# One row of each partition of a block stored by itself, in transfers of 125 and 3 partitions that only the first five DMA engines move

## The chip, the cores and the metric

The kernel runs on one core of a Trainium2 chip. The metric is the time of the kernel on the device in microseconds (us), lower is better. Times are medians over several executions, and a comparison uses executions of both kernels on the same chip in the same rounds. The ratios given are the mean time of the fast runs of one kernel over that of the other's of the same rounds, so they are not quite the ratios of the medians that stand beside them.

## The reference

A linear layer with an adapted and normalized weight (DoRA), in float32; `x` has 16 x 2048 rows of 256 numbers and `W` is 256 x 256:

```python
W_adapted = W + scale * (lora_A @ lora_B)
W_norm = np.sqrt(np.sum(W_adapted ** 2, axis=0, keepdims=True) + 1e-8)
W_final = W_adapted / W_norm * m
y = x.reshape(-1, in_dim) @ W_final
```

Nearly all of the cost is reading `x` (33.6 MB) and writing `y` (33.6 MB).

## The kernel before

The rows of `x` are cut into 8 blocks of 4096. A block lies in SBUF as 128 partitions with 32 rows of 1 KB each, in one of five buffers. Loads go out from SyncE (SP), stores from ScalarE (ACT); each of the two issues into a queue of its own, and both queues run on the same 16 DMA engines. A chunk is 4 rows of each partition. GpSimd rounds two chunks to bfloat16, TensorE transposes and multiplies, VectorE and ACT empty the accumulators, and ACT writes `y` over the chunk of `x` and issues a store when enough chunks are done.

The stores, as (first chunk, chunks, rows in one transfer, chunk after whose drain it is issued); here `F` is 3, `G` is 24, `CH` is 8 and `J` is 4:

```python
stores = [(b * CH, CH, CH * J, 19 + b) for b in range(F - 1)]
stores += [(G - CH, 3, 3 * J, G), (G - 5, 5, 5 * J, G)]
FIRST = len(stores)
stores += [(G, 4, J, G + 3), (G + 4, 1, J, G + 4)]
stores += [(G + 5, CH - 5, (CH - 5) * J, 44), (G + CH, CH, CH * J, 44)]   # the first of these is changed
stores += [(b * CH, CH, CH * J, (b + 1) * CH - 1) for b in range(F + 2, NBLK - 1)]
stores += [(g0, cnt, cnt * J, g0 + cnt - 1) for g0, cnt in units[-2:]]
# ... (cut)
for r in range(0, cnt * J, rows):                                          # in transfer()
    here = x_bufs[b % XBUFS][:, c * J + r : c * J + r + rows, :]
    there = unit[:, (g0 - u0) * J + r : (g0 - u0) * J + r + rows, :]
    src, dst = (here, there) if store else (there, here)
    engine.dma_start(out=dst, in_=src).then_inc(sem(name), 16)
```

## Time and profile before

| | before |
|---|---|
| time, median | 162.64 us (162.43 to 163.18, 3 runs) |
| span of the profiled execution | 161.3 us |
| moved | 33.85 MB read, 33.55 MB written, 418 GB/s on the mean |
| compute ends (last store issued) | 131.15 us |
| last byte of the last store | 160.74 us |

The kernel is bound by its transfers: the DMA engines are full from start to end, and the last 30 us are stores that wait in the queue. Its time is therefore the time at which the last of the 16 DMA engines is done. The lines that show this are in the prediction below.

### The profile page before, as it was taken

How to read it: one execution, taken by the hardware profiler on the slowest of the kernel's cores; microseconds unless marked ns; L12 is line 12 of the kernel's file. 1: busy time of each engine (PE TensorE's matmuls, PEld its weight loads, DVE VectorE, ACT ScalarE, POOL GpSimd, SP SyncE). 2: the span in 40 equal slices, each digit the busy share in tenths (PEclk: the TensorE clock that was granted, in tenths of full speed). 3: DMA queues.
4: the chain of work that ended last, by engine and by line, in shares of the span. 5: the costliest groups of instructions: out<-in, count | busy, mean ns of one | idle time of the engine just before them, and what ended most of it. 6: DMA issues, size and time to landing. Idle time of an engine off the chain costs nothing. (4 is left out here: it accounts for less than half of the span.)

```text
span 161.3 us, 2027 instructions
## 1 busy us (share of the span) xinstructions
PE 96.0 (60%) x786; PEld 84.8 (53%) x786; DVE 45.0 (28%) x44; ACT 66.0 (41%) x68; POOL 60.9 (38%) x38
## 2 busy tenths in 40 slices
PE   0795936999999720000799999989997920000000
PEld 0384925899998610000689999979977910000000
DVE  0667421435353500000214445335443300000000
ACT  3311740686777450000057676777774640000000
POOL 1045319668685000002938676755829000000000
PEclk9999996999999985555569999999999997555555
DMA  4999999999999999989999999999999999999995
GB/s 167 425 457 455 390 512 398 390 512 398 423 390 480 398 463 426 431 365 453 423 403 444 407 437 427 422 423 430 443 483 398 423 473 408 406 480 415 386 443 219
DMA packets 4645, 67.43 MB, mean 418 GB/s; under 512 B 657, under 2 KB 674, under 8 KB 1698
## 3 DMA queue, kind: packets, MB, share of 16 engines
q1 hardware_dynamic: 2304, 33.82, 49.2%
q10 hardware_dynamic: 2338, 33.59, 48.9%
q14 instruction: 3, 0.02, 0.0%
HBM read 33.85 MB, written 33.55 MB: 418 GB/s over the span
## 5 line engine op out<-in xcount | busy, mean ns | idle before, releaser
L276 ACT COPY x_sb<-y_ps 128x1024 f32<-128x1024 f32 x64 | 62.2, 1015 | 58.8 <-PE y_ps L335 57.1
L208 POOL CAST xb<-x_sb 128x2048 bf16<-128x2048 f32 x31 | 58.4, 1893 | 63.5 <-DMA x_sb<-in_x_dram 24.8
L335 PE MATMUL y_ps<-w_final,xt 128*128 128x256 bf16 x512 | 64.1, 279 | 3.9 <-PEq L311 3.8
L248 DVE COPY xt<-xt_ps 128x1024 f32<-128x1024 f32 x32 | 39.1, 1224 | 75.1 <-PE xt_ps L321 75.0
L335 PEld LDWEIGHTS y_ps<-w_final,xt 128*128 128x128 bf16 x512 | 51.0, 100 | 11.5 <-issue 4.9
L321 PE MATMUL xt_ps<-identity,xb 128*128 128x128 f32 x264 | 37.5, 290 | 24.9 <-PEq L311 24.9
L321 PEld LDWEIGHTS xt_ps<-identity,xb 128*128 128x128 f32 x264 | 32.8, 151 | 26.4 <-issue 25.9
L292 PE MATMUL y_ps<-identity,a_nat 128*16 128x128 f32 x2 | 0.6, 398 | 4.2 <-DMA a_nat<-in_lora_A_dram 4.2
L264 ACT CAST xb<-x_sb 128x2048 bf16<-128x2048 f32 x1 | 1.9, 1898 | 2.6 <-DMA x_sb<-in_x_dram 2.6
L292 PEld LDWEIGHTS y_ps<-identity,a_nat 128*16 128x16 f32 x2 | 0.1, 88 | 4.1 <-issue 4.1
L262 ACT ACT_TABLE_LOAD x1 | 1.3, 1283 | 2.4 <-issue 2.4
L238 DVE RECIPROCAL rnorm<-norm 128x256 f32<-128x256 f32 x1 | 1.8, 1752 | 1.3 <-ACT norm L268 1.3
L305 PE MATMUL y_ps<-sq,ones 128*128 128x256 f32 x4 | 2.1, 675 | 0.0
L214 POOL MEMSET xb<- 128x2048 bf16 x1 | 1.8, 1805 | 0.0
L305 PEld LDWEIGHTS y_ps<-sq,ones 128*128 128x128 f32 x4 | 1.2, 324 | 0.8 <-DVE sq L229 0.7
L301 PE MATMUL y_ps<-m_row,ones 1*128 1x256 f32 x2 | 1.2, 710 | 0.5 <-DMA m_row<-in_m_dram 0.5
L220 DVE CAST b_bf<-b_nat 16x256 bf16<-16x256 f32 x1 | 0.3, 281 | 3.3 <-DMA b_nat<-in_lora_B_dram 3.3
L301 PEld LDWEIGHTS y_ps<-m_row,ones 1*128 1x128 f32 x2 | 0.5, 305 | 1.0 <-DMA m_row<-in_m_dram 1.0
L268 ACT ACTIVATE norm<-y_ps,eps_col 128x256 f32<-128x256 f32 x1 | 0.5, 476 | 1.2 <-PE y_ps L305 1.2
L225 DVE SCALAR_TENSOR_TENSOR wa<-y_ps,w_nat 128x512 f32<-128x512 f32 x1 | 0.7, 692 | 0.8 <-PE y_ps L296 0.8
L296 PE MATMUL y_ps<-b_bf,aT 16*128 16x256 bf16 x2 | 0.6, 400 | 0.5 <-DVE aT L222 0.5
L241 DVE TENSOR_TENSOR w_final<-wam,rnorm 128x256 bf16<-128x256 f32 x2 | 0.8, 422 | 0.0
(14 smaller groups left out, 3.7 us busy)
## 6 DMA issues: line engine op xcount, KB each, us to landing
out_dram<-x_sb ACTq DMA_DIRECT2D x5, 4096.0 KB, 27.2
x_sb<-in_x_dram SPq DMA_DIRECT2D x7, 2048.0 KB, 29.6
x_sb<-in_x_dram SPq DMA_DIRECT2D x3, 4096.0 KB, 29.9
out_dram<-x_sb ACTq DMA_DIRECT2D x2, 2048.0 KB, 30.3
x_sb<-in_x_dram SPq DMA_DIRECT2D x1, 3072.0 KB, 46.1
out_dram<-x_sb ACTq DMA_DIRECT2D x2, 1536.0 KB, 19.3
out_dram<-x_sb ACTq DMA_DIRECT2D x1, 2560.0 KB, 30.7
out_dram<-x_sb ACTq DMA_DIRECT2D x5, 512.0 KB, 38.1
```

The source lines that it names most:

```text
L208: nc.gpsimd.tensor_copy(out=xb_bufs[p % NXB][:], in_=x_bufs[b % XBUFS][:, 2 * c * J : 2 * (c + 1) * J, :],).then_inc(sem("rounded"), 1)
L214: nc.gpsimd.memset(xb_bufs[NPR % NXB][:], 0.0).then_inc(sem("rounded"), 1)
L238: nc.vector.reciprocal(out=rnorm[:], in_=norm[:]).then_inc(dv, 1)
L241: i = nc.vector.tensor_mul(out=w_final[:, t], in0=wam[:, t], in1=rnorm[:])
L248: nc.vector.tensor_copy(out=xt_bufs[p % NXT][:].rearrange("p r t -> p (r t)").bitcast(FP32), in_=xt_ps[p % 2][:],).then_inc(sem("copied"), 1)
L262: nc.scalar.activation(out=warm[:], in_=eps_col[:], func=AF.Sqrt)
L264: nc.scalar.copy(out=xb_bufs[0][:], in_=x_bufs[0][:, 0 : 2 * J, :]).then_inc(sem("early"), 1)
L276: nc.scalar.copy(out=x_bufs[b % XBUFS][:, c * J : (c + 1) * J, :], in_=y_ps[g % 2][:]).then_inc(sem("room"), 1)
L301: nc.tensor.matmul(mb_ps, ones[0:1, :], m_row[:], start=True, stop=True).then_inc(pe, 1)
L305: i = nc.tensor.matmul(n2_ps, ones[:], sq[:, t, :], start=(t == 0), stop=(t == KC - 1))
L321: i = nc.tensor.transpose(xt_ps[p % 2][:, j * P : (j + 1) * P], xb_bufs[p % NXB][:, j, :].bitcast(FP32), identity[:],)
L335: i = nc.tensor.matmul(y_ps[h][:, j, :], xt_bufs[p % NXT][:, r : r + P, t], w_final[:, t, :], start=(t == 0 and (j % (J // 2)) == 0), stop ...
```

## The change

Its intent is to even out the ends of the DMA engines. The store of the last three chunks of block 3 has 12 rows in each partition. The twelfth row is taken out of it and stored in two transfers, of partitions 0 to 124 and 125 to 127. A transfer of 125 partitions is moved by five engines only, one of 3 partitions by three, so 128 KB that all 16 engines shared now lie on the first five.

```diff
+    ODD = FIRST + 2
...
     def pieces(entry):
+        if entry is stores[ODD]:
+            return 16 * 3
         return 16 * (entry[1] * J // entry[2])
...
-            engine.dma_start(out=dst, in_=src).then_inc(sem(name), 16)
+            parts = [(0, P, 0, rows)]
+            if (g0, cnt, rows) == stores[ODD][:3]:
+                parts = [(0, P, 0, rows - 1), (0, 125, rows - 1, 1), (125, 3, rows - 1, 1)]
+            for p0, n, r0, k in parts:
+                engine.dma_start(
+                    out=dst[p0 : p0 + n, r0 : r0 + k, :],
+                    in_=src[p0 : p0 + n, r0 : r0 + k, :],
+                ).then_inc(sem(name), 16)
```

## The prediction

> **What bounds the kernel now.** I read the page first: the span, the forty slices, the DMA queues and the chain that ended last.
>
> ```profile
> span 161.3 us, 2027 instructions
> ...
> PE   0795936999999720000799999989997920000000
> ...
> DMA  4999999999999999989999999999999999999995
> GB/s 167 425 457 455 390 512 398 390 512 398 423 390 480 398 463 426 431 365 453 423 403 444 407 437 427 422 423 430 443 483 398 423 473 408 406 480 415 386 443 219
> ...
> HBM read 33.85 MB, written 33.55 MB: 418 GB/s over the span
> ```
>
> The 16 DMA engines are full from the second slice to the last but one. TensorE is empty in the last seven slices, so compute is done at about 131 us and the last 30 us are stores alone. The chain that ended last covers only a few per cent of the span for the same reason: the thing waited for at the end is a queue of transfers. The kernel moves 67.4 MB and cannot be shorter than the time in which its most loaded DMA engine moves its sixteenth. So for this change the only question is which DMA engine ends last, and by how much.
>
> Next I read the tail in a table of windows. The two columns that matter are the last two: mean share of the 16 engines that is busy, and GB/s. A packet is counted in the window in which it starts, so one of 1 us can show more than 1.00.
>
> ```profile
> 157.00:158.00 1.00, 0.00 (x0) 0.00 (x0) 0.00 (x0) 0.00 (x0) 0.00 (x0) 0.50 0.92 393
> 158.00:159.00 1.00, 0.00 (x0) 0.00 (x0) 0.00 (x0) 0.00 (x0) 0.00 (x0) 0.50 1.11 475
> 159.00:159.50 0.50, 0.00 (x0) 0.00 (x0) 0.00 (x0) 0.00 (x0) 0.00 (x0) 0.50 0.39 164
> 159.50:160.00 0.50, 0.00 (x0) 0.00 (x0) 0.00 (x0) 0.00 (x0) 0.00 (x0) 0.50 0.08 33
> 160.00:161.30 1.30, 0.00 (x0) 0.00 (x0) 0.00 (x0) 0.00 (x0) 0.00 (x0) 0.50 0.03 13
> ```
>
> In the last window 0.03 x 1.3 us x 16 engines = 0.62 us: a single packet of 16 KB (611 ns each in the trace) on a single engine. All other engines are already empty. So there is a **straggler**, one of sixteen.
>
> To size it I used the packet records of the trace (start, duration, bytes; the engine is not recorded). In steady state a packet starts 3 or 4 ns before the previous packet of the same engine ends, and each engine must get its share of every transfer in order, so the records can be linked into 16 chains. This is my reconstruction, but it leaves almost no gap unexplained. The chains end at 159.26, 159.30, 159.31, 159.34, 159.35, 159.40, 159.45, 159.49, 159.49, 159.50, 159.65, 159.71, 159.74, 159.99, 160.02 and 160.74 us; the mean is 159.61. Perfect balance would therefore be worth 160.74 - 159.61 = 1.13 us (0.7% of 162.64), which caps any gain from moving bytes between engines. The straggler's lead over the next is 0.72 us. Its 32 KB store packets averaged 1240 ns against the normal 1213 ns, in long runs of slow packets (49 to 57 us and 116 to 136 us); it is slow again and again, not hit once. The two at 160.0 got there by a few isolated long packets or by one 303 ns gap. The chain that also carried the one-partition load of m ends at 159.35.
>
> **What the Trainium skill says.** "DMA: Bandwidth & Descriptors", section "Why a DMA increments its semaphore by 16 and not by 1": a transfer issued from SP or ACT uses the largest k up to 16 that divides the slowest dimension, on the lowest-numbered k engines; the unused 16 - k increments come at once. So 125 partitions go to engines 0 to 4 with 25 rows each, and 3 partitions to engines 0 to 2 with one each. The wait for 3 x 16 remains right. The trace of before has only even transfers and the one-partition load, so it shows no more than that this load's 1 KB packet was one packet. The same page, "Latency and other measured facts": engines 7 and 15 are usually slower than the rest in traces, with a guess at a cause tied to the software path. The trace agrees that one engine is slow in the stores (1240 against 1213 ns) though nothing here uses that path; it can't tell which number it has. The same page, "Why small descriptors are slow": each packet has a fixed overhead. The trace agrees: a 1 KB packet takes 46 ns, 4 KB takes 159, 12 KB takes 460, 16 KB takes 611; that is about 37.7 ns per KB plus 8 ns.
>
> **The change part by part.** The transfer concerned is the store of the last three chunks of block 3 (12 rows of 1 KB in each partition, 1.5 MB), issued when the 45th chunk is drained.
>
> ```profile
> 104.49 0.86 ACTq L146 DMA_DIRECT2D out_dram<-x_sb  x2
> 104.80 0.86 PEld L335 LDWEIGHTS y_ps<-w_final,xt 128*128 128x128 bf16 x8
> ...
> 105.39 1.93 ACT L276 COPY x_sb<-y_ps 128x1024 f32<-128x1024 f32 x2 [1.01 <-ACTq L282]
> ...
> 119.86 1.89 POOL L208 CAST xb<-x_sb 128x2048 bf16<-128x2048 f32 x1 [3.75 <-DMA x_sb<-in_x_dram]
> ...
> 121.90 1.06 PE L321 MATMUL xt_ps<-identity,xb 128*128 128x128 f32 x8 [1.22 <-PEq L311]
> ...
> 131.15 0.34 ACTq L146 DMA_DIRECT2D out_dram<-x_sb  x1
> ```
>
> *Removed, on all 16 engines:* eight packets of 12 KB become eight of 11 KB. At 37.7 ns per KB an 11 KB packet is about 422 ns, so each engine gives back 8 x (460 - 422) = 0.30 us. Engines 5 to 15 keep this.
>
> *Added, on engines 0 to 4:* 25 packets of 1 KB, at 46 - 4 = 42 ns from start to start: 1.05 us, plus some 6 ns for the completion write. Engines 0 to 2 get one more packet and completion, 0.05 us. Net: 1.06 - 0.30 = +0.76 us on engines 3 and 4, +0.81 us on 0 to 2. In total the engines work 5 x 0.78 - 11 x 0.30 = +0.6 us more, 0.04 us each on the mean, for the small packets' overhead; bytes are the same.
>
> *Moved to the end:* these packets run at 115 to 121 us, and behind them each engine's store queue is full without a gap until 160 us. An engine's saving or loss therefore arrives whole at its own end. If the straggler is among 5 to 15 it ends at 160.74 - 0.30 = 160.44 us. Engine 0, if it is the chain with the load of m, ends at 159.35 + 0.81 = 160.16. A typical chain (159.3 to 159.5) among 1 to 4 ends at 160.1 to 160.3, still before the straggler. So the best result is a shorter span by 0.30 us.
>
> *Added on ACT:* two more DMA issues at about 0.43 us each (0.86 us for two in the line above). The copies behind them, and TensorE, which waits for the room they make, slide by up to 0.9 us. That is **off the path**: POOL waits 3.75 us for a load at 119.86 and TensorE idles 1.22 us before 121.90, which swallows it. Even if it did not, the last store is issued at 131.15 us into a queue that has 29 us of work ahead. The store issued at 108.74 us starts moving only at about 120.6 us. Loads share the engines by turns with the stores at this time; the change can shift a load by some tenths of a us, again ahead of 29 us of queued stores.
>
> Sum: -0.30 us if only the straggler decides.
>
> **The rivals.** *First: another engine takes the end.* The two chains at 160.0, if among engines 1 to 4, would end at 160.8 and give a result of 0 to +0.1 us; chains at 159.71 and 159.74 there would end at about 160.5, a gain of only 0.2 us. Four of fourteen drawn blindly would include one of the two latest about half the time. For it: the margins are below 0.8 us. Against it: those two were late by isolated events that needn't fall on the same engines again, and the number five was chosen with 0.8 us of room. This rival makes the time 162.5 to 162.75.
>
> *Second: the straggler is itself among the first five.* Then it gets +0.8 us and ends at 161.5: 163.4 us. Against it: the skill's page puts the slow ones at 7 and 15, and the chain with the load of m, which has to be engine 0 by that page, isn't it. I give it 6%.
>
> *Third: the one-row transfer costs more than its packets.* 25 rows on one engine with a stride of 32 KB in DRAM, and reads from SBUF that leave the usual split of partitions, might run slower than 46 ns each. At double the time engines 0 to 4 would gain 1.9 us and end at 161.2 to 161.4, which makes 163.1 to 163.3 us. The 1 KB loads at the start (46 ns each) speak against it, but were single packets.
>
> *Fourth: the straggler is not stable.* If it is slow by a different amount in each run, a saving of 0.30 us drowns: the three times before already span 162.43 to 163.18, 0.75 us. The mechanism would then be right and not visible in medians.
>
> **Range and chances.** Full gain: 162.64 - 0.30 = 162.34. Weighted with the first rival (about half the time, some 0.2 us less gain) and small shares of the second and third (+0.7 us each at 5%): about 162.4 to 162.5; I choose 162.4. The scatter of before is +0.5/-0.2 us around its median, so 162.0 to 162.9 should hold it 8 times in 10. Faster by 2% would need 3.25 us, three times what perfect balance gives: 1%. Slower by 2% would need engines 0 to 4 to lose some 4 us, five times the sum: 1%. Within 2%: 98%.
>
> **What would show each step.** In the packet records: 128 packets of 11 KB at about 422 ns in place of half of the 12 KB ones, and 128 packets of 1 KB more at about 46 ns; two completions more on each of the first three engines and one more on the next two. In the linked chains: five ends later by about 0.8 us against the others, the straggler earlier by 0.3 us, and a tail whose last window holds several engines instead of one. On the timeline, four issues from ACT at about 104.5 us taking some 1.7 us, the later issues up to 0.9 us late, and the final one still near 131 us. The prediction is wrong if the slow chain is one of the five, if 1 KB packets take well over 46 ns in a row, or if the time moves by more than 1 us either way.

## More of the kernel before

TensorE runs its part in a loop of 16 turns; the other engines' instructions stand one after the other in the program.

One more line of the page, not read closely at the time, matters later. It is of the part on DMA queues: queue and kind, then packets, MB, and share of the 16 engines' time.

```profile
q14 instruction: 3, 0.02, 0.0%
```

Three packets of 8 KB that no transfer of the kernel asked for: the engines' own instructions, brought in by DMA.

## The result, and the profile after

The changed kernel took 163.51 us (median of 6 runs, 163.27 to 164.18) against 162.60 us for the kernel before (6 runs, 162.43 to 163.18). The ratio is 1.0056, with a 95% interval of 1.0032 to 1.0081. This is a small but clear loss, where a gain of 0.24 us was predicted; it lies outside the predicted range. In a second comparison on another occasion (experiment 2) the ratio was 1.0031 (1.0008 to 1.0055), so the sign is settled and the size is 0.4 to 0.9 us.

The page after, span and DMA queues:

```profile
span 161.9 us, 2029 instructions
...
q10 hardware_dynamic: 2474, 33.59, 48.8%
q14 instruction: 3, 0.02, 0.0%
```

The store queue (q10) has 136 packets more than the 2338 of before: the 128 rows of 1 KB and 8 completions more (two on each of three engines, one on two). The bytes and the three instruction blocks are the same.

The timeline after, where the changed store is issued and where compute meets its loads (start, duration, engine, what, and in brackets the idle time before it):

```profile
103.28 1.55 ACTq L156 DMA_DIRECT2D out_dram<-x_sb  x4
104.88 1.93 ACT L289 COPY x_sb<-y_ps 128x1024 f32<-128x1024 f32 x2 [1.71 <-PE y_ps L348]
...
119.94 3.73 POOL L221 CAST xb<-x_sb 128x2048 bf16<-128x2048 f32 x2 [3.67 <-DMA x_sb<-in_x_dram]
...
131.23 0.34 ACTq L156 DMA_DIRECT2D out_dram<-x_sb  x1
```

Four issues took 1.55 us where two took 0.86, GpSimd waited 3.67 us for the same load as before (3.75), and the last store left ACT at 131.23 us (131.15 before). The extra work on ACT cost nothing, as expected. The loss is in the tail. The table of windows after (last two columns: busy share of the 16 DMA engines, GB/s):

```profile
159.00:159.50 0.50, 0.00 (x0) 0.00 (x0) 0.00 (x0) 0.00 (x0) 0.00 (x0) 0.50 0.54 229
159.50:160.00 0.50, 0.00 (x0) 0.00 (x0) 0.00 (x0) 0.00 (x0) 0.00 (x0) 0.50 0.39 164
160.00:160.50 0.50, 0.00 (x0) 0.00 (x0) 0.00 (x0) 0.00 (x0) 0.00 (x0) 0.50 0.23 98
160.50:161.00 0.50, 0.00 (x0) 0.00 (x0) 0.00 (x0) 0.00 (x0) 0.00 (x0) 0.50 0.08 33
```

At 16 KB and 0.61 us a packet, 0.39 x 0.5 x 16 = 3.1 us is five packets started from 159.5 to 160.0 us, 0.23 is three from 160.0 to 160.5 and 0.08 one from 160.5 to 161.0. So several engines are late and one of them is last, where before one engine was alone. That one ends 0.7 us later than the straggler did.

Linking the packet records into the 16 chains, as the prediction did, names them (chain ends in us; the rows of 1 KB that a chain moved tell which class of engines it is: 26 rows are engines 0 to 2, 25 are engines 3 and 4, none are engines 5 to 15):

| chain | end before | end after |
|---|---|---|
| eleven without rows | not told apart | 159.07 to 159.98 |
| 26 rows, also carried the load of `m` (engine 0) | 159.35 | 160.56 |
| 26 rows, instruction block at 136 us | 159.65 or 159.74 | 160.61 |
| 25 rows, instruction block at 131 us | 159.99 | 160.89 |
| 26 rows, instruction block at 86 us | 159.71 | 160.99 |
| 25 rows, slow store packets | 160.74 | 161.42 |

(In the trace of before two packets start in the same nanosecond behind the block at 136 us, so two links fit. The longer of the two packets follows the block in the other traces, which speaks for 159.74.)

The straggler was one of the five. Its 32 KB store packets from 118 us on averaged 1239 ns after and 1241 before; the normal packet is 1213. Three more of the five are the engines that bring in the instruction blocks, and these were the 303 ns gaps that the prediction had seen without knowing what they were: in the packet records of before, the three packets of queue 14 start at 86.92, 131.44 and 136.30 us and take 309 ns each, just where those chains have their gaps. In the chain of the block at 131 us the store packet beside it was also longer by about 350 ns, in both traces.

The ends of two traces can't be compared to the tenth of a us. The mean of the 16 ends is 159.88 us here, 0.27 later than before, where 0.04 was worked out; in the trace of experiment 1, whose load is even, it is 159.96. What the change did is better read from the five against the eleven: the mean of the five ends lay 0.4 us behind that of the eleven before (with 159.74 for the block at 136 us) and lies 1.5 us behind it after, 1.0 us more, where some 0.8 + 0.3 was worked out.

### The profile page after: what moved, and what is told of

It is laid out like the page before. It is cut to its first block, busy times and chain, and to the rows that moved or that the text cites. A ratio compares the mean times of both kernels' runs of the same rounds, so it can differ in the third digit from the quotient of the medians.

```text
span 161.9 us, 2029 instructions
## 1 busy us (share of the span) xinstructions
PE 95.1 (59%) x786; PEld 84.0 (52%) x786; DVE 44.9 (28%) x44; ACT 66.2 (41%) x68; POOL 60.8 (38%) x38
## 5 line engine op out<-in xcount | busy, mean ns | idle before, releaser
L334 PE MATMUL xt_ps<-identity,xb 128*128 128x128 f32 x264 | 37.0, 288 | 25.4 <-PEq L324 25.4
L334 PEld LDWEIGHTS xt_ps<-identity,xb 128*128 128x128 f32 x264 | 32.3, 149 | 26.8 <-issue 26.3
```

The costliest lines, as they stand in the source:

```text
L334: i = nc.tensor.transpose(xt_ps[p % 2][:, j * P : (j + 1) * P], xb_bufs[p % NXB][:, j, :].bitcast(FP32), identity[:],)
```

## The experiments

Theory A: the change made the kernel slower since the engine that ends last anyway is one of the first five; it ends later by what it was given. Theory B: storing a row by itself, in small packets and more transfers, is what costs, whoever moves it. Theory C: which engine is late is a matter of the run or the chip. All experiments gave correct results. Experiments 1 to 5 edit the changed kernel, 6 and 7 the kernel before; the first group of four ran on the same chip and shared its runs of before (162.91 us median, 11 runs).

### 1. The row by itself, on all 16 engines

```diff
-                parts = [(0, P, 0, rows - 1), (0, 125, rows - 1, 1), (125, 3, rows - 1, 1)]
+                parts = [(0, P, 0, rows - 1), (0, P, rows - 1, 1)]
```

> The twelfth row is stored by itself again, but as one transfer of 128 partitions, so all 16 DMA engines take 8 rows of 1 KB each. The packets are as small as in the change and ACT issues one transfer more than before; only the uneven share is gone. Theory A (the first five DMA engines hold the one that ends last, and the change gave it 25 rows): each engine gains 8 x 42 ns - 0.30 us = some 0.03 us, so the time is that of before, 162.6 to 162.7, ratio 0.999 to 1.002. Theory B (a row stored by itself in small packets, and more transfers issued, costs 0.9 us whoever moves it): ratio near 1.005, 163.4 us or so.

Measured: 162.89 us (6 runs), ratio 1.0007 (0.9985 to 1.0028). In the windows of the tail a single engine is again alone, as before the change:

```profile
160.00:160.50 0.50, 0.00 (x0) 0.00 (x0) 0.00 (x0) 0.00 (x0) 0.00 (x0) 0.50 0.08 33
160.50:161.00 0.50, 0.00 (x0) 0.00 (x0) 0.00 (x0) 0.00 (x0) 0.00 (x0) 0.50 0.00 0
```

The last chain ends at 160.76 us, with slow packets of 1239 ns on the mean, against 160.74 before. Theory B falls: small packets and one more transfer (the change has two more) cost nothing that can be seen. What is left is the uneven share.

### 2. The changed kernel once more

No edit. It ran with the two kernels of experiment 5; before took 162.99 us (11 runs).

> The changed kernel once more, on whatever chip this call gets, to see whether the cause stays where it is. Theory A (engine 4 is slow in the stores and engines 1 to 3 each carry one hidden gap of 303 ns, in every run): the five chains with 25 or 26 rows of 1 KB are again the last five, the last of all has 25 rows, the gaps near 87, 131 and 136 us lie on three of the other four; the time is 0.8 to 1.0 us over that of before, ratio 1.004 to 1.007. Rival (which engine is late is a matter of the run or the chip): another chain is last, or the ratio is within 0.002 of 1.

Measured: 163.42 us (6 runs), ratio 1.0031 (1.0008 to 1.0055), a little under what was expected. The five chains with rows are again the last five, at 160.42 (26 rows), 160.81 (26, block at 136 us), 160.99 (25, block at 131 us), 161.00 (26) and 161.69 us (25); all others end by 159.74. The last has 25 rows, and its 32 KB packets issued after 110 us averaged 1240 ns. The block at 87 us lies ahead of the stretch that could be linked here, so its chain was not confirmed. (A second linking, which holds each transfer to eight packets on an engine, puts it on the chain of 26 rows that ends at 161.00 us or, 5 ns from it, 160.99 us.) Theory C falls for what decides the end: the late engine is the same one in both traces of this kernel, as far as its rows tell. It was no test of another chip: chip 9 for this run and for the first group. Experiments 6 and 7, on chip 15, show a chain with the same slow packets.

### 3. Twice the dose, and a dose for the first three alone

```diff
-                parts = [(0, P, 0, rows - 1), (0, 125, rows - 1, 1), (125, 3, rows - 1, 1)]
+                parts = [(0, P, 0, rows - 2), (0, 125, rows - 2, 2), (125, 3, rows - 2, 2)]
```

> The last two rows of each partition go in the transfers of 125 and 3 partitions, so the first five DMA engines take 25 packets of 2 KB: the same number of transfers and packets as in the change, twice the bytes. Theory A: a 2 KB packet is about 84 ns (80 from start to start), the eight packets of 10 KB give back 8 x 76 = 0.6 us, so the engine that ends last gains 25 x 0.08 - 0.6 = 1.4 us in place of the change's 0.76: about 164.0 to 164.2 us, ratio 1.009 to 1.010. In the linked chains the last one again carries the 25 packets, and the eleven other engines end 0.6 us earlier than before. Theory B (a cost for each small packet or transfer, not for bytes): as the change, about 163.5 us, ratio 1.005 to 1.006.

Measured: 163.92 us (4 runs), ratio 1.0063 (1.0035 to 1.0091), 1.0 us more than before. A said a ratio of 1.009 to 1.010 and B 1.005 to 1.006; the measured value lies between, and its interval reaches both, so the times alone do not decide. The trace does. Its span is 162.7 us, 1.4 us over that of before, and the last window holds two packets (0.05 x 1.7 us x 16 = 1.4 us):

```profile
161.00:162.70 1.70, 0.00 (x0) 0.00 (x0) 0.00 (x0) 0.00 (x0) 0.00 (x0) 0.50 0.05 19
```

The packets of 2 KB follow each other every 80 ns on five chains. The last chain has 25 of them and the slow store packets (1241 ns), and ends at 162.19 us: 1.45 us after the straggler of before, 1.4 expected. Ten of the eleven chains without rows end at 158.7 to 159.1 us. The lateness grows with the bytes given to that engine, not with the number of transfers.

```diff
-                parts = [(0, P, 0, rows - 1), (0, 125, rows - 1, 1), (125, 3, rows - 1, 1)]
+                parts = [(0, P, 0, rows - 1), (0, 123, rows - 1, 1), (123, 5, rows - 1, 1)]
```

> The twelfth row goes in transfers of 123 and 5 partitions: engines 0 to 2 take 41 + 1 rows, engines 3 and 4 one row, the others none. Theory A with the slow engine at 3 or 4: the slow one ends at 160.74 - 0.30 + 0.05 = 160.5 us and is no longer the last; engines 0 to 2 gain 42 x 42 ns + 0.01 - 0.30 = 1.5 us and end at about 161.2 to 161.7 (from 159.75, 159.8 and 160.2, their ends in the changed kernel less 0.8). The time is then 163.2 to 163.6 us, with the last chain having 42 rows. If instead the slow engine is one of 0 to 2, it ends at 162.2 us and the time is 164.1 us. Theory B: about 163.5 us as in the change.

Measured: 163.01 us (4 runs), ratio 1.0011 (0.9984 to 1.0038): better than the 163.2 to 163.6 expected, in the trace as expected. The slow chain has one row and ends at 160.46 us (160.5 expected), which is 0.28 us earlier than before; it is no longer last. The three chains with 42 rows end at 160.82, 161.26 and 161.27 us, at the lower edge of what was expected, and a chain without rows at 161.02, for which I have no reason. So the slow engine is 3 or 4. That it ends 0.28 us earlier, as the prediction would have it, is one trace, and such an end differs by more than that from trace to trace (see experiment 5). The engines that are given the bytes in its place end later than it did.

### 4. A marker for each engine

```diff
-                parts = [(0, P, 0, rows - 1), (0, 125, rows - 1, 1), (125, 3, rows - 1, 1)]
+                parts = [(0, P, 0, rows - 1), (120, 8, rows - 1, 1)]
+                parts += [(sum(range(n + 1, 16)), n, rows - 1, 1) for n in range(15, 0, -1)]
```

> A marker. The twelfth row is stored in 16 transfers of 8, 15, 14, 13 ... 1 partitions. If n partitions (n below 16) use the n lowest engines with a row each, engine e moves 15 - e rows, and one more for e below 8, so each engine shows a number of 1 KB packets of its own and every chain of the trace can be given its number. Theory A: the chain that ends last is number 3 or 4 (the last chain of the changed kernel had 25 rows and no more), and the 303 ns gaps lie on engines below 5 too. It carries 12 or 13 rows, so it gains about 13 x 48 ns - 0.30 = 0.3 us and the time is 162.8 to 163.0 us; the 7 us that ACT needs for issuing 16 transfers stay hidden in front of the stores queued. Rival: the late chain has another number, above 4, or another one than in the changed kernel, and the change lengthened the tail in another way.

Measured: 164.73 us (4 runs), ratio 1.0108 (1.0074 to 1.0143). The numbers came out, the time did not. The five latest chains are, by their rows, engines 0 to 4: they end at 161.46 to 161.76 us, and the last, with the long run of slow packets, at 162.78 us with 12 rows, which makes it engine 4. The chain with the instruction block that was at 131 us has 13 rows, engine 3. (Rows of 42 ns let neighbouring chains be swapped in the linking: two ways of linking agree on these two, but differ by a few rows on some others. The class of 25 or 26 rows in experiments 2 and 3 is not open to this.)

The time is 1.8 us over before where 0.2 to 0.4 was expected. In the trace, eight chains, the first five among them, took 1.5 to 2.1 us in place of 1.2 for a 32 KB packet once or twice between 121 and 124 us, right after the small transfers. Why is open; it says that 16 small transfers in a row cost more than their packets. A useful thing came with it. ACT needed 6.72 us for its issues, and compute ended some 6.2 us later:

```profile
104.21 6.72 ACTq L157 DMA_DIRECT2D out_dram<-x_sb  x18
...
137.38 0.34 ACTq L157 DMA_DIRECT2D out_dram<-x_sb  x1
```

Two of the three instruction blocks moved with it, from 131.4 to 137.9 and from 136.3 to 142.8 us, as did the end of the slow packets, from 132.8 to 138.3 us (one more packet, 33 ns over the normal, starts at 139.7). So both go with the progress of compute, not with the clock or with the bytes.

### 5. The row issued by GpSimd, to get it onto the other eleven

ACT stores the first 11 rows (in a second kernel 10) as one transfer of 128 partitions. The rest goes in transfers of 5, 121 and 2 partitions from GpSimd's own queue, after a wait for the drain of its chunk, each on a semaphore of its own:

```diff
+            nc.gpsimd.wait_ge(sem("done"), 6)
+            for (p0, n), s in zip([(0, 5), (5, 121), (126, 2)], row_sems):
+                nc.gpsimd.dma_start(
+                    out=there[p0 : p0 + n, last - 1 : last, :],
+                    in_=x_bufs[b6 % XBUFS][p0 : p0 + n, last - 1 : last, :],
+                ).then_inc(s, 16)
```

> The inverse of the change, tried from the GpSimd queue[...]: the twelfth row goes in transfers of 5, 121 and 2 partitions issued by GpSimd. If these take 5, then the next 11, then 2 engines, the eleven engines 5 to 15 get 11 rows each and the first five 1 or 2. Theory A then: engine 4 ends 0.25 us earlier (160.74 to 160.5), the eleven gain 11 x 42 ns - 0.30 = 0.16 us and stay in front of it, so the time falls by some 0.25 us, ratio 0.998 to 0.999. If the 121 partitions are spread nearly evenly instead (8 rows on most engines), it is a control as the even row was: ratio 0.999 to 1.002. If what counts is only that the row is stored by itself, 1.005.

> The same with two rows. If the 121 partitions go to engines 5 to 15, engine 4 ends some 0.5 us earlier (0.60 given back, 0.08 to 0.16 taken), the eleven gain 11 x 80 ns - 0.60 = 0.28 us and end at 159.6 to 160.3 in the trace: ratio 0.996 to 0.998, faster than before by 0.4 us and than the change by 1.3 us. If they are spread nearly evenly: 0.999 to 1.002.

Measured: 163.23 us, ratio 1.0017 (0.9991 to 1.0042), and for two rows 163.03 us, ratio 1.0015 (0.9988 to 1.0042). Beside the changed kernel of the same rounds (163.42 us) that is no clear gain, beside before no clear loss. The packets tell why it is no inverse of the change. In the packet records of the one-row kernel, the 121 rows are 30 packets of 4 KB (four rows each, 159 ns) and one packet of 1 KB. That is 8 rows on each of 15 engines and one on the last: nearly even. The queue's line:

```profile
q0 software_dynamic: 112, 0.13, 0.2%
```

So this was a second control, and agrees with the first. In its trace the chain with the slow packets is last again, at 161.29 us, though its load is even; in experiment 1 it ended at 160.76. So the end of the slow engine differs by half a us between two traces in which it got no more than the others. Theory A's inverse, unloading the first five, was not reached. Of what I tried, no version beats the kernel before.

### 6. TensorE's loop written out

Why is engine 4 slow? The slow packets stop with compute, so a guess was that TensorE's instructions are brought in through it, in small pieces, at each turn of the loop.

```diff
-    with nc.Fori(0, NPR // 2, 1, engines=[PE], head_slot={PE: 128}):
+    for _ in range(NPR // 2):
```

> The kernel before (no odd row) with TensorE's loop of 16 turns written out, so each TensorE instruction stands in the program once. The slow engine is slow only while compute runs: its last long packet starts about 1 us after the last drain in every run (132.8 for compute until 131.2 us; 138.3 for 137.4 in the ladder). Theory F: it is slow since TensorE's instructions are brought in through it in small pieces while the loop turns. Written out, the long run of packets stretched by 50 to 120 ns should go or change its form (whole gaps of 303 ns as on engines 1 to 3, some 15 of them for about 1,900 instructions, up to 4.5 us on one engine and a time of 165 to 166 us; or none, and then 160.0 in place of 160.74 as the last end and 162.0 to 162.3 us). Rival: the slowness has nothing to do with the loop; the same run of stretched packets, 160.7 us as the last end, ratio 0.998 to 1.002.

Measured: 163.33 us (4 runs), ratio 1.0045 (1.0020 to 1.0069), against 162.84 us before. The guess falls: the slow packets are there as before, 33 to 102 ns over the normal packet, from 122 to 134 us and in two more up to 137.7, with compute until 135.9 us. What is new is a queue of instruction blocks for TensorE:

```profile
q8 instruction: 6, 0.10, 0.2%
```

Each of the six blocks of 16 KB takes 0.92 to 1.02 us on a chain of its own, and the chain with the block at 37 us is now the last, at 161.50 us (it was also hit by a packet stretched by 0.85 us at 49 us). The slow chain ends at 160.79. So an instruction block is work for a DMA engine like any other. Here one block and one long packet together set the end; neither alone was tested.

### 7. More instructions in each turn of the loop

```diff
         turned(0)
         product(1)
+        for _ in range(32):
+            nc.tensor.wait_ge(sem("ident"), 1)
```

> The kernel before with 32 more waits on a semaphore long reached in each turn of TensorE's loop (about 120 instructions before). Theory F: the slow engine has a quarter more to bring in, so its stretch of 1.4 us over the other engines grows to some 1.8 us and its end moves from 160.7 to about 161.1 us; ratio 1.002 to 1.004, if the turns do not get so long that the last stores come late. Rival: the stretch depends on how long compute runs, not on the number of instructions, or not on TensorE at all: stretched packets of the same 50 to 120 ns, and an end that moves only if compute takes longer.

Measured: 163.27 us (4 runs), ratio 1.0029 (1.0011 to 1.0047), so the time that the guess asked for; but the reason in the trace is the rival's. Compute lasts until 140.3 us, the slow packets do too (the last at 141.9), and each is stretched by 23 to 99 ns, no more than before. They are only more: stretches of up to 200 ns after 119 us sum to 1.32 us against 0.69 in before. The slow chain ends at 161.42 us, and two chains without this pattern end after it, at 161.69 and 161.77, with long packets at 78 and 118 us (the linking of this trace breaks off at 53 us, so their whole history isn't known). The slowness of engine 4 lasts as long as compute runs beside stores, and does not depend on the number of TensorE's instructions. What it is remains open.

## Why the prediction was wrong

**The bound, the cap and the tail: right.** The kernel's time is the end of the last DMA engine, and the change altered only how they end. Perfect balance was said to be worth 1.13 us at most; the loss is of the same order. That lateness put on a saturated engine at 120 us arrives whole at 160 us was right: the slow chain ended 0.68 us later in the changed kernel and 1.45 us later with two rows, where 0.76 and 1.4 us were worked out for 25 packets. That the numbers agree so closely is in part luck: the same chain ended at 160.74, 160.76 and 161.29 us in three traces with an even or nearly even load (before, experiment 1, one row from GpSimd). That lateness grows with the dose does not rest on it: between the mean of the five ends and that of the eleven, the distance grows from 0.4 us before to 1.5 after and in the repeat and to 2.5 with two rows.

**The cost of each packet: right.** The 11 KB packets took 422 ns, as estimated, and the 1 KB packets 46 ns, one every 42 ns in a row. The third rival, that a row in five pieces runs slower, is refuted by the same numbers.

**The work on ACT: right.** It was 1.55 us for four issues (1.7 said), absorbed where said.

**Which engines: wrong, and this decided.** The step that failed is the one that put the straggler among engines 5 to 15, so that it would keep the 0.30 us it gives back and end at 160.44 us. It carried 25 rows and ended at 161.42 us. So the second rival came true, "the straggler is itself among the first five", which was given 6% and should have had far more. Its working was right (163.4 us said, 163.51 measured). Two arguments held it down. One was the Trainium skill's page "DMA: Bandwidth & Descriptors", section "Latency and other measured facts", which puts the usually slower engines at 7 and 15. That is a remark on traces of another kind, with a guess at a cause tied to the software queue that this kernel does not use, and it doesn't hold here: the slow chain has 25 rows, so it is engine 3 or 4, and 12 rows in the ladder, so 4. The other was that the chain with the load of `m` was not the slow one; that rules out engine 0 only.

Without that page, a blind draw would have given 4 in 15, about 27%, for the straggler to be one of engines 1 to 4. And then the first rival stood beside it: the chains at 159.65 (or 159.74), 159.71 and 159.99 us, all with a gap of 303 ns. The prediction called these isolated events "that needn't fall on the same engines again". They are instruction blocks, and they fall on chains with rows after, in the repeat and in the experiment with two rows (all three blocks after, those near 131 and 136 us in all three traces; the trace of before has no rows to tell classes by). The page had the count of them in one line, and the packet records had their times. Had the two been laid together, four of the six latest chains would have been seen to be late by a block or by slow packets, which come again in every trace here, and none of them could be counted on to have 0.8 us of room.

**The fourth rival**, that the straggler changes from run to run, is refuted by experiments 1, 2 and 3: the same pattern of slow packets shows in each. Over the normal 1213 ns, the chain's last 24 store packets of 32 KB sum to 0.63 to 0.73 us in all of these traces and in those of before and after. Whether the pattern is there without the profiler can't be seen and was not tested: the record gives a span and a granted clock for every timed run. The times show a loss of the same size as the spans (0.9 and 0.4 us in the two comparisons, 0.6 us between the two spans).

**What stays open:** why engine 4 is slow while compute runs (and that it is 4 and not 3 rests on the ladder alone); why the ladder cost 1.8 us; and whether unloading the first five would gain the 0.3 us that the straggler's part promises. No transfer tried from ACT loaded other engines alone (those of fewer than 16 engines lay on nested sets of five and three), and the attempt through GpSimd spread evenly.

## What to carry to other kernels

When a kernel is bound by full DMA queues, its time is the end of one DMA engine, and a balance between engines has to be made from the measured end of each, by its number; which engine ends last must be marked and measured before bytes are moved to "the others". Here the transfers of 125 and 3 partitions loaded five and three engines, and these are the ones that already carry the instruction blocks and the slow stores, so it was the wrong side to add to. An argument from a general remark about slow engines is weaker than one extra run with a marker.

## What the Trainium skill lacked or had wrong

- "DMA: Bandwidth & Descriptors", "Latency and other measured facts", says that engines 7 and 15 are usually slower. Here the slow engine is one of the first five, number 4 by the marker. Its 32 KB store packets took 1240 ns on the mean against 1213, the long ones only while compute ran beside stores, and without any use of the software queue, to which the page ties its guess at a cause.
- "Runtime: NRT & Kernel Launch", "Instruction fetch mechanics", has the blocks at 16 KiB and the cost of a boundary as mostly hidden. That speaks of the engine that executes them. The DMA engine that carries a block pays for it: here each of three blocks of 8 KB took 0.31 us of one, and TensorE's loop written out added six of 16 KB at 0.92 to 1.02 us each. With full queues this is not hidden: a chain with such a block, and one long packet, ended last, at 161.50 us against 160.74. No page says which DMA engines carry them; here it was engines among the first five for the 8 KB blocks, and a different engine for each of the six.
- "DMA: Bandwidth & Descriptors", "Why a DMA increments its semaphore by 16 and not by 1", was right on both of its rules: 125 partitions went to five engines with 25 rows each, and 121 partitions from GpSimd to 15 engines with 8 rows and one with a single row. It has no figure for what small transfers in a row cost beside full queues: 16 of them came with 1.8 us of added time, of which their packets explain 0.3.
